# Second feed-forward projection of an encoder block: eight dense quarter products against seven block products

## The chip, the cores and the metric

The kernel runs on one core of one Trainium2 chip. The metric is device time in microseconds (us): the median of three timed runs. A separate execution was recorded by the hardware profiler; its page and its trace are what is read here.

TensorE (PE) multiplies a 128x128 stationary tile (loaded by PEld) with a moving tile of up to 512 columns into PSUM banks. VectorE (DVE), ScalarE (ACT) and GpSimd (POOL) work elementwise. SyncE's queue (SP) issues nearly all DMAs; a few are issued by ACT's queue.

## The reference, cut to what matters

One layer of a hybrid encoder on 1024 tokens of width 1024: an input layer norm, a wide projection, dilated attention and a gated recurrence, a merge, layer norm 1, and a SwiGLU feed-forward part with layer norm 2. The change lies in the last line and a half:

```
gate, up = jnp.split(h @ w_ffn_in[l], 2, axis=-1)
h = layer_norm(DEEPNORM_ALPHA * h + (jax.nn.silu(gate) * up) @ w_ffn_out[l], ln2_g[l], ln2_b[l])
```

The hidden width D_FF is 2816, which is 22 tiles of 128 (`NF`). The second projection therefore multiplies a 1024 x 2816 matrix (tokens by hidden) with a 2816 x 1024 matrix. All of it is float32.

## The kernel before

**Numbers in halves.** Each float32 operand is split into a high part rounded to the matmul's type and a low part that is the remainder (`split`: a cast on ACT, a subtraction on POOL or DVE). `mm3` then makes one product of three matmuls: high by high, high by low, low by high (lines 225, 226, 227 in the kernel before).

**First projection (`ffn_in`).** It makes the 22 hidden tiles one after the other, each for all 1024 tokens, by a seven-product block scheme (`wino_project`) of 7 x 4 x 3 = 84 matmuls per tile. An `evac` function turns the finished banks into the gated values `c` (tile `fc`), splits them (`fgh`, `fgl`) and stores both parts to DRAM (`gd`).

**Second projection (`ffn_out`).** It is dense. For the first four token tiles, eight PSUM banks (four tiles by two column halves) accumulate over all 22 hidden tiles; for each hidden tile `out_weights` loads a 512 KB row block of the weights into `w_raw` and splits it into `wohi`, `wolo`, which stay in SBUF, and `out_acts` loads the two stored parts of the activations (`gwsum`, `gwkeep`). For the last four token tiles the weights are there, and only activations are loaded. That makes 22 x 8 x 2 x 3 = 1056 matmuls. `finish` adds the banks to the residual row block `y` (loaded from `ahs`), takes the layer norm, and stores the output.

**Order.** The code is written as a stream of operations on tiles from rotating pools; a scheduler then sets each engine's instruction order ahead of time, by its own model of durations and by priorities. On the chip every engine runs its list strictly in order, and SP issues its DMAs strictly in order. A load is stopped at the queue's head until its buffer is free, and everything behind it waits too. The DMAs use eight completion semaphores in turn, so that at most eight are under way.

**Names.** `gwsum`, `gwkeep`: activations, high and low part, before. `Wb_...`: a 128x512 block of the weights, after. `graw`, `ghi`, `glo`: activations raw, high, low, after. `a22h`, `a22l`: high and low part of the last block's activations, after. `y`: residual rows, `ahs`: their copy in DRAM. `ga11f`, `gs4h` and the like: activation blocks in DRAM, after.

Of the kernel before, what the change touches and what calls it, by code (L numbers as in the profile page):

```python
# [25 lines left out]
NF = D_FF // 128  # L26
ALPHA = 2.0 ** 0.25
# [52 lines left out]
class Block:  # L80
    evac_ahead = 1000

    def __init__(self, ctx, tc, x, ln_in_g, ln_in_b, w_in, hgrn_lb, hgrn_norm_g, w_att_up, w_hgrn_up,
# [35 lines left out]
        self.gd = [[dram.tile([128, 4, T], F32, name=f"gd{i}{z}") for z in ("hi", "lo")] for i in range(6)]  # L119
# [1018 lines left out]
    def phase2(self):  # L1138
        nc = self.nc
        gc, bc = self.col["g1"], self.col["b1"]  # L1140
        with ExitStack() as es:
# [69 lines left out]
            for t in range(8):  # L1211
# [31 lines left out]
                if t in (5, 6):  # L1243
                    raws.append(self.ffn_raws(t - 5))
# [126 lines left out]
    def ffn_in(self):  # L1371

        nc = self.nc
        with ExitStack() as es:
# [3 lines left out]
            self.fp = fp = es.enter_context(self.pool("ffn", "right"))  # L1378

            def evac_of(f):  # L1380
                c, th = (fp.tile([128, T], F32, name=n, tag=n, bufs=2) for n in ("fc", "fth"))
                gh, gl = (fp.tile([128, T], F32R, name=n, tag=n, bufs=2) for n in ("fgh", "fgl"))

                def evac(i, l, ps, add):
# [11 lines left out]
                    self.split(gh[:, s], gl[:, s], c[:, s], eng_lo="dve")  # L1396
                    for t, d in zip((gh, gl), self.gd[f // 4]):
                        nc.sync.dma_start(d[:, f % 4, s], t[:, s].bitcast(F32))

                return evac  # L1400

# [5 lines left out]
            self.first_evac = [evac_of(f) for f in range(2)]  # L1407
            for i, n in enumerate(("b22", "t3", "t4")):
                for k in (0, 2):
                    tag = "fgh" if k else "fgl"  # L1410
                    r = fp.tile([128, 2, HALF], F32, name="t_raw", tag=tag, bufs=2)
                    nc.sync.dma_start(r, self.td[i][:, k:k + 2, :])
                    hi, lo = self.xb[n]
                    self.split(hi[:, k:k + 2, :], lo[:, k:k + 2, :], r, eng_lo="dve")
            ab = []
            held = None
            for f in range(NF):
                if f > 1:
                    grp = self.wino_project(nxt, evac_of(f))
                    next(grp)  # L1420
                else:
                    grp = self.first_groups[f]
                if 1 < f + 1 < NF:
                    nxt = self.ffn_raws(f + 1)
                if held:
                    next(held, None)
                next(grp)
                held = grp
                if f == 3:
                    for v in self.ln["1"]:  # L1430
                        vecs(v)
                if 5 <= f < 21 and f % 2:
                    t = f // 2 - 2
                    n = fp.tile([128, D], F32, name="res", tag="fc", bufs=2)
# [9 lines left out]
    def out_weights(self, f):  # L1444

        r = self.wraw.tile([128, D], F32, name="w_raw", tag="wraw", bufs=2)
        self.nc.sync.dma_start(r, self.wfo[128 * f:128 * (f + 1), :])
        if f < 2:
            t = [[z.rearrange("p k c -> p (k c)") for z in self.granules()] for _ in range(2)]
        else:  # L1450
            z = [self.fob.tile([128, D], F32R, name=f"wo{n}{f}") for n in ("hi", "lo")]
            t = [[y[:, HALF * h:HALF * (h + 1)] for y in z] for h in range(2)]
        for h, (hi, lo) in enumerate(t):
            self.split(hi, lo, r[:, HALF * h:HALF * (h + 1)], eng_lo="dve" if h else "pool")
        return t

    def out_acts(self, f, tk, n=4):

        out = []
        for i, tag in enumerate(("wsum", "wkeep")):  # L1460
            t = self.ws.tile([128, 4, 128], F32R, name=f"g{tag}", tag=tag, bufs=3)
            d = self.gd[f // 4][i]
            if tk.stop - tk.start == HALF:
                self.nc.sync.dma_start(t.rearrange("p k c -> p (k c)").bitcast(F32), d[:, f % 4, tk])
            else:
                self.nc.sync.dma_start(t[:, :n, :].bitcast(F32), d[:, 0:n, tk])
            out.append(t)
        return out

    def ffn_out(self):  # L1470
# [3 lines left out]
        with ExitStack() as es:  # L1474
            self.fob = es.enter_context(self.pool("fob"))
            rp = es.enter_context(self.pool("for", "right"))
            g2, b2 = (rp.tile([128, D], F32, name=n) for n in ("g2", "b2"))
            for t, v in zip((g2, b2), self.ln["2"]):
                nc.scalar.dma_start(t, bass.AP(tensor=v.tensor, offset=v.offset, ap=[[0, 128], [1, D]]))

            def finish(t, banks):
                y = rp.tile([128, D], F32, name="y2", tag="y2", bufs=2)
                nc.sync.dma_start(y, self.ahs_d[t])
                halves = [slice(HALF * h, HALF * (h + 1)) for h in range(2)]
                for s, ps in zip(halves, banks):
                    nc.vector.tensor_add(y[:, s], y[:, s], ps)
# [88 lines left out]
```

## Time and profile before

| | |
|---|---|
| Three runs | 2162.01, 2162.53, 2163.58 us; median 2162.53 |
| Profiled execution | span 2160.4 us from first to last instruction; its run time is not given apart, and the median of the runs is 2.1 us above the span |
| TensorE busy, share of the span | 2058.8 us, 95% |
| DVE, ACT, POOL busy | 1266.4, 883.3, 1108.9 us |
| DMA | 306.87 MB, mean 142 GB/s |
| Mean granted TensorE clock | 0.987 |

How to read it: busy times are sums over the whole span, and they say little about one stage. The second projection is the last tenth of the span, so the windows from about 1900 us on are the ones that bear on the change. The first projection fills about 1500 to 1911 us.

### The profile page before, as it was taken

The numbers are of one execution on the slowest core, as the hardware profiler recorded it, in microseconds if no ns is written. First come the engines' busy times: TensorE is split into PE (matmuls) and PEld (weight loads), VectorE is DVE, ScalarE is ACT, GpSimd is POOL, SyncE is SP. The second block draws the span as 40 slices with busy tenths as digits, with TensorE's granted clock in tenths as the row PEclk, the third lists the DMA queues.
The fourth block names the chain that finished last, engine by engine and source line by source line (L and its number), as shares of the span: only waits on it lengthen the run. The fifth ranks groups of instructions, "written<-read, shape, count | busy, mean of one in ns | idle before, by whom it ended". The sixth has DMA issues, their size and how long they took to land.

```text
span 2160.4 us, 31020 instructions
## 1 busy us (share of the span) xinstructions
PE 2058.8 (95%) x11073; PEld 1700.5 (79%) x11073; DVE 1266.4 (59%) x2037; ACT 883.3 (41%) x1798; POOL 1108.9 (51%) x905
## 2 busy tenths in 40 slices
PE   4799999999999999989999899998999999999998
PEld 3678887778878888778888688786888888887886
DVE  8667646876459854768446623247766776743221
ACT  6534455444544436444364431244444444432000
POOL 3565553566436763656635864443665666633120
PEclk9899999999999999999999999999999999999999
DMA  6343442434334453333525774245334444376452
GB/s 209 99 126 103 144 148 90 145 118 159 118 95 141 136 167 100 127 118 127 166 91 183 238 227 132 88 142 174 132 123 135 148 135 137 123 233 215 132 171 87
DMA packets 291644, 306.87 MB, mean 142 GB/s; under 512 B 14689, under 2 KB 222882, under 8 KB 291490
## 3 DMA queue, kind: packets, MB, share of 16 engines
q1 hardware_dynamic: 283744, 278.45, 40.7%
q10 hardware_dynamic: 7746, 26.45, 3.1%
q8 instruction: 87, 1.43, 0.3%
q14 instruction: 67, 0.55, 0.1%
HBM read 203.13 MB, written 101.71 MB: 141 GB/s over the span
## 4 chain that ended last, share of the span: by engine, by line
PE 61%; DVE 5%; DMA 4%; POOL 3%; issue 3%; ACT 1%; SPq 0%; DVEq 0%; POOLq 0%; ACTq 0%
PE pj L225 13%; PE pj L226 12%; PE pj L227 12%; PE sd L225 6%; PE sd L227 6%; PE sd L226 6%; POOL w_lo L204 2%; DMA w_raw<-in_w_ffn_out_dram 2%; PE sd L1019 1%; DVE hR L980 1%; DVE wolo L204 1%; DVE hR L979 1%; ACT wohi L200 0%; PE sd L557 0%; DMA wa<-in_w_in_dram 0%
## 5 line engine op out<-in xcount | busy, mean ns | idle before, releaser
L204 POOL TENSOR_TENSOR w_lo<-wa,w_hi 128x512 fp32r<-128x512 f32 x276 | 385.7, 1405 | 276.3 <-ACT w_hi L200 260.9
L200 ACT CAST w_hi<-wa 128x512 fp32r<-128x512 f32 x276 | 170.1, 618 | 231.7 <-PE pj L226 164.7
L204 POOL TENSOR_TENSOR w_lo<-wsum,w_hi 128x512 fp32r<-128x512 f32 x88 | 120.5, 1380 | 133.5 <-ACT w_hi L200 81.9
L225 PE MATMUL pj<-xt1hi,w_hi 128*128 128x512 f32 x268 | 109.1, 408 | 22.9 <-ACT xt1hi L200 15.3
L204 POOL TENSOR_TENSOR w_lo<-f_raw,w_hi 128x512 fp32r<-128x512 f32 x66 | 99.8, 1514 | 52.6 <-ACT w_hi L200 50.2
L226 PE MATMUL pj<-xt1lo,w_hi 128*128 128x512 f32 x268 | 107.9, 403 | 4.5 <-DVE xt1lo L204 4.5
L227 PE MATMUL pj<-xt1hi,w_lo 128*128 128x512 f32 x268 | 107.1, 400 | 0.0
L227 PE MATMUL pj<-xb22hi,w_lo 128*128 128x512 f32 x268 | 104.8, 391 | 1.8 <-POOL w_lo L204 1.8
L225 PE MATMUL pj<-xb22hi,w_hi 128*128 128x512 f32 x268 | 105.7, 394 | 0.4 <-ACT wkeep L1341 0.4
L226 PE MATMUL pj<-xb22lo,w_hi 128*128 128x512 f32 x268 | 104.9, 391 | 0.0
L459 POOL TENSOR_TENSOR wa<-wa,wa 128x512 f32<-128x512 f32 x46 | 65.4, 1422 | 72.4 <-DVE ws L458 61.0
L194 POOL TENSOR_TENSOR mv<-mv,mhalf 128x1 f32<-128x1 f32 x24 | 16.5, 689 | 162.8 <-DVE mv L193 159.6
L204 POOL TENSOR_TENSOR w_lo<-ws,w_hi 128x512 fp32r<-128x512 f32 x46 | 67.3, 1467 | 63.5 <-ACT w_hi L200 59.5
L200 ACT CAST w_hi<-wsum 128x512 fp32r<-128x512 f32 x88 | 54.6, 620 | 102.1 <-PE sd L226 67.2
L481 ACT COPY wkeep<-pj 128x512 f32<-128x512 f32 x138 | 80.4, 582 | 11.5 <-DVE evh L373 6.0
L225 PE MATMUL pj<-xb11hi,w_hi 128*128 128x512 f32 x188 | 77.6, 414 | 4.7 <-DVE wkeep L398 3.1
L225 PEld LDWEIGHTS pj<-xt1hi,w_hi 128*128 128x128 f32 x268 | 51.7, 194 | 36.7 <-ACT xt1hi L200 15.9
L225 PE MATMUL pj<-xt4hi,w_hi 128*128 128x512 f32 x188 | 75.8, 403 | 3.9 <-DVE evh L373 3.9
L384 DVE TENSOR_TENSOR evh<-wkeep,pj 128x512 f32<-128x512 f32 x48 | 32.7, 680 | 76.5 <-PE pj L227 56.3
L227 PE MATMUL pj<-xt2hi,w_lo 128*128 128x512 f32 x188 | 73.9, 393 | 3.3 <-POOL w_lo L204 3.3
L971 ACT ACTIVATE hS<-hR,dec 128x128 f32<-128x128 f32 x112 | 44.5, 402 | 79.4 <-DVE hR L980 56.3
L226 PE MATMUL pj<-xb11lo,w_hi 128*128 128x512 f32 x188 | 75.7, 403 | 1.0 <-DVE xb11lo L204 1.0
(396 smaller groups left out, 6517.7 us busy)
## 6 DMA issues: line engine op xcount, KB each, us to landing
wa<-in_w_in_dram SPq DMA_DIRECT2D x184, 256.0 KB, 3.1
f_raw<-in_w_ffn_in_dram SPq DMA_DIRECT2D x44, 512.0 KB, 4.1
w_raw<-in_w_ffn_out_dram SPq DMA_DIRECT2D x22, 512.0 KB, 3.6
tg<-evh SPq DMA_DIRECT2D x32, 256.0 KB, 3.0
tg<-tg SPq DMA_DIRECT2D x16, 512.0 KB, 3.8
y<-ahs SPq DMA_DIRECT2D x16, 512.0 KB, 3.7
ah<-xt ACTq DMA_DIRECT2D x8, 512.0 KB, 6.7
rec<-hg ACTq DMA_DIRECT2D x8, 512.0 KB, 3.6
```

Source lines behind the costliest of these rows:

```text
L200: nc.scalar.copy(hi, src)
L204: e.tensor_sub(lo, src, hi.bitcast(F32))
L225: nc.tensor.matmul(ps, whi, xhi, start=first, stop=False, **kw)
L226: nc.tensor.matmul(ps, whi, xlo, start=False, stop=False, **kw)
L227: nc.tensor.matmul(ps, wlo, xhi, start=False, stop=last, **kw)
L384: nc.vector.tensor_add(t, add, ps)
L459: nc.gpsimd.tensor_sub(a["a21"], a["a11"], a["a21"])
L481: nc.scalar.copy(t, ps)
L971: nc.scalar.activation(S[:, c, :], E, AF.Copy, scale=dec[:, 1, c:c + 1])
L979: nc.vector.scalar_tensor_tensor(En, E, dec[:, 1, c:c + 1], ps[:, jj, :], op0=OP.mult, op1=OP.add)
L980: nc.vector.tensor_scalar(En, En, dec[:, 0, c:c + 1], None, op0=OP.mult)
L1019: nc.tensor.matmul(po[:, jj, :], l, r, start=(n == 0), stop=(n == len(terms) - 1))
```

## The change

The dense second projection is replaced by a seven-product block scheme, like that of the first projection. The activations are seen as 2 x 2 blocks (hidden tiles j and j + 11, token halves), the weights too, and the 22 hidden tiles become 11 pairs (`NJ`). Seven products over 11 pairs, each for four token tiles and 512 columns, make 7 x 11 x 4 x 3 = 924 matmuls.

- `ffn_in` now makes the hidden tiles in the order 0, 11, 1, 12, ... (`FS`), so that a pair is complete after two. A new `combine` makes the four block sums of the activations: `s3` (POOL) after the first tile of a pair, `s1`, `s2`, `s4` (DVE) after the second. It stores `a11`, `a12`, `s2` whole and `s3`, `a22`, `s1`, `s4` as two parts: 11 stores of 256 KB per pair where there were 8.
- The last three tables of the first projection (`b22`, `t3`, `t4`) are fetched in 12 loads of 256 KB instead of 6 of 512 KB.
- `ffn_out` runs the products in the order 1, 2, 6, 5, 7, 3, 4. Every one but the last takes 11 steps of 12 matmuls. Products 1, 6, 7 and 4 use one set of four banks (`X`, the `pj` banks), 2, 5 and 3 the other (`Z`, the `sd` banks).
- All 44 weight blocks stay in SBUF as raw float32; `right` forms the sums of weights in place on DVE, and each step splits its weight block anew (ACT and POOL). `a11`, `a12`, `s2` are loaded raw and split on arrival; `s1`, `s3`, `s4` are loaded as two parts.
- All eight `y` rows stay in SBUF, and after each product the banks are added straight into them.

```diff
-            self.first_out = self.out_weights(0), self.out_acts(0, slice(0, HALF))
             next(held, None)
+            combine(NJ - 1, 1)
...
+            def combine(j, second):
+                a11, a21 = (C[j][:, HALF * l:HALF * (l + 1)] for l in range(2))
+                if not second:
+                    whole("a11", j, a11)
+                    s3 = small("s3")
+                    nc.gpsimd.tensor_sub(s3, a11, a21)
+                    parts("s3", j, s3)
+                    return
+                a12, a22 = (C[j + NJ][:, HALF * l:HALF * (l + 1)] for l in range(2))
+                whole("a12", j, a12)
+                parts("a22", j, a22)
+                s1, s2, s4 = (small(n) for n in ("s1", "s2", "s4"))
+                nc.vector.tensor_add(s1, a21, a22)
+                nc.vector.tensor_sub(s2, s1, a11)
+                nc.vector.tensor_sub(s4, a12, s2)
...
+    OUT_ORDER = (1, 2, 6, 5, 7, 3)
...
+            def acts(p, j):
+                d = self.gd[self.OUT_G[p]][j]
+                z = [rp.tile([128, HALF], F32R, name=f"g{n}", tag=f"g{n}", bufs=3) for n in ("hi", "lo")]
+                if len(d) == 1:
+                    r = self.ws.tile([128, HALF], F32, name="graw", tag="wsum", bufs=3)
+                    nc.sync.dma_start(r, d[0])
+                    self.split(*z, r, eng_lo="dve")
+                else:
+                    for t, s in zip(z, d):
+                        nc.sync.dma_start(t.bitcast(F32), s)
+                return z
+
+            def right(p, j):
...
+                if p == 6:
+                    t2 = self.ws.tile([128, HALF], F32, name="wt2", tag="wkeep", bufs=3)
+                    nc.vector.tensor_sub(b11, b12, b11)
+                    nc.vector.tensor_sub(t2, b22, b11)
+                    return t2
...
+            for j in range(NJ):
+                load("b11", j)
...
+            for p in self.OUT_ORDER:
+                bank = X if p in (1, 6, 7) else Z
+                for j in range(NJ):
+                    if p == 1:
+                        load("b21", j)
+                        if j in (3, 5, 7, 9):
+                            rows((j - 3) // 2)
+                    if p == 2:
+                        load("b12", j)
...
+                    g = acts(p, j)
+                    w = self.granules()
+                    w = [z.rearrange("p k c -> p (k c)") for z in w]
+                    self.split(*w, right(p, j))
...
+                    for t in range(4):
+                        c = slice(128 * t, 128 * (t + 1))
+                        self.mm3(bank[t], g[0][:, c], g[1][:, c], *w, p in (1, 2, 5) and j == 0, j == NJ - 1,
+                                 skip_group_check=True)
...
+            for t in range(4):
+                for j in range(NJ):
+                    self.mm3(X[t], a22[t][0][:, j, :], a22[t][1][:, j, :], *late[j], False, j == NJ - 1,
+                             skip_group_check=True)
+                add(4 + t, 0, X[t])
+                finish(t)
             for t in range(4, 8):
+                finish(t)
```

The order of the instructions moves with it. Three places matter for what follows.

SP's queue at the end of the first projection, before: the first activations and weights of the second projection stand between the last stores (`gd5hi`, `gd5lo`) of the first.

```order
L1398 DMA gd5hi<-fgh 128x512
L1398 DMA gd5lo<-fgl 128x512
L1464 DMA gwsum<-gd0hi 128x512 x2
L1398 DMA gd5hi<-fgh 128x512
L1398 DMA gd5lo<-fgl 128x512
L1464 DMA gwkeep<-gd0lo 128x512
L1447 DMA w_raw<-in_w_ffn_out_dram 128x1024
```

The same place after, where `gs1h`, `gs2f`, `gs1l`, `ga12f`, `gs4h` are stores of the last pair:

```order
L1414 DMA gs1h_255<-gh 128x512
L1408 DMA gs2f_234<-s_17476 128x512
L1414 DMA gs1l_256<-gl 128x512
L1408 DMA ga12f_223<-fc 128x512
L1493 DMA Wb_17504<-in_w_ffn_out_dram 128x512
L1493 DMA Wb_17506<-in_w_ffn_out_dram 128x512
L1414 DMA gs4h_299<-gh 128x512
```

Three activation loads (`graw` of steps 0 to 2) stand ahead of this piece, but the first weight block now stands behind the store `ga12f_223`, whose data comes from the very last product of the first projection.

SP's queue some 15 us into the second projection, before: two loads of weights and two of activations take turns.

```order
L1447 DMA w_raw<-in_w_ffn_out_dram 128x1024 x2
L1464 DMA gwsum<-gd1hi 128x512
L1464 DMA gwkeep<-gd1lo 128x512
L1447 DMA w_raw<-in_w_ffn_out_dram 128x1024 x2
L1464 DMA gwsum<-gd1hi 128x512
```

The corresponding stretch after, from the activations of step 8 (`ga11f_210`) to those of step 9 (`ga11f_211`):

```order
L1504 DMA graw<-ga11f_210 128x512
L1493 DMA Wb_18246<-in_w_ffn_out_dram 128x512
L1493 DMA Wb_18273<-in_w_ffn_out_dram 128x512
L1497 DMA y_18400<-ahs_119 128x1024
L1497 DMA y_18444<-ahs_120 128x1024
L1497 DMA y_18488<-ahs_121 128x1024
L1497 DMA y_18532<-ahs_122 128x1024
L1597 DMA a22h<-ga22h 128x11x128
L1597 DMA a22l<-ga22l 128x11x128
L1597 DMA a22h<-ga22h 128x11x128
L1597 DMA a22l<-ga22l 128x11x128
L1504 DMA graw<-ga11f_211 128x512
```

The last two of the 44 weight blocks, the rows of the second token half (asked for by the code in product 5) and half of the activations of product 4 have moved ahead of the activations of step 9 of product 1.

DVE's list near the start of the second projection, before: subtractions of weights (`wolo`), which wait only for their own block.

```order
L204 TENSOR_TENSOR fgl<-fc,fgh 128x512
L204 TENSOR_TENSOR wolo_17317<-w_raw,wohi_17316 128x512
L204 TENSOR_TENSOR wolo_17353<-w_raw,wohi_17352 128x512
L204 TENSOR_TENSOR wolo_17389<-w_raw,wohi_17388 128x512
L204 TENSOR_TENSOR wolo_17425<-w_raw,wohi_17424 128x512
```

DVE's list after, from a sum of weights for product 6 (line 1519) to the low part of the activations of step 6 of product 1 (`glo`):

```order
L1519 TENSOR_TENSOR Wb_17520<-Wb_18002,Wb_17520 128x512
L1520 TENSOR_TENSOR wt_18094<-Wb_18004,Wb_17504 128x512
L1526 TENSOR_TENSOR Wb_17810<-Wb_18004,Wb_17810 128x512
L1519 TENSOR_TENSOR Wb_17522<-Wb_18028,Wb_17522 128x512
L1520 TENSOR_TENSOR wt_18121<-Wb_18030,Wb_17506 128x512
L1526 TENSOR_TENSOR Wb_17834<-Wb_18030,Wb_17834 128x512
L208 TENSOR_TENSOR glo<-graw,ghi 128x512
```

The sums for products 6 and 7 have moved into product 1, and a `glo` behind them waits until their weight blocks have landed.

More of the change, by code (lines that the diff above doesn't have):

```diff
@@ L26 @@
 NF = D_FF // 128
+NJ = NF // 2
+FS = [j + NJ * z for j in range(NJ) for z in range(2)]
 ALPHA = 2.0 ** 0.25
@@ L118, in __init__ @@
         self.td = [dram.tile([128, 4, HALF], F32, name=f"td{i}") for i in range(3)]
-        self.gd = [[dram.tile([128, 4, T], F32, name=f"gd{i}{z}") for z in ("hi", "lo")] for i in range(6)]
+        self.gd = {n: [[dram.tile([128, HALF], F32, name=f"g{n}{z}{j}") for z in zs] for j in range(NJ)]
+                   for n, zs in (("a11", "f"), ("a12", "f"), ("s2", "f"), ("s1", "hl"), ("s3", "hl"), ("s4", "hl"))}
+        self.gd["a22"] = [dram.tile([128, NJ, HALF], F32, name=f"ga22{z}") for z in "hl"]
         self.consts()
@@ L1378, in ffn_in @@
             self.fp = fp = es.enter_context(self.pool("ffn", "right"))
+            C = {}
             def evac_of(f):
-                c, th = (fp.tile([128, T], F32, name=n, tag=n, bufs=2) for n in ("fc", "fth"))
-                gh, gl = (fp.tile([128, T], F32R, name=n, tag=n, bufs=2) for n in ("fgh", "fgl"))
+                C[f] = c = fp.tile([128, T], F32, name="fc", tag="fc", bufs=4)
+                th = fp.tile([128, T], F32, name="fth", tag="fth", bufs=2)
                 def evac(i, l, ps, add):
@@ L1438, in ffn_in @@
                     nc.scalar.dma_start(self.ahs_d[t], n)
-            self.first_out = self.out_weights(0), self.out_acts(0, slice(0, HALF))
             next(held, None)
+            combine(NJ - 1, 1)
         self.rawpool.__exit__(None, None, None)
         self.h1p.__exit__(None, None, None)
[L1444 to L1468, printed above, removed]
+    OUT_ORDER = (1, 2, 6, 5, 7, 3)
+    OUT_G = {1: "a11", 2: "a12", 6: "s2", 5: "s1", 7: "s3", 3: "s4"}
     def ffn_out(self):
@@ new lines, in ffn_out, with load, rows @@
+            halves = [slice(HALF * h, HALF * (h + 1)) for h in range(2)]
+            def load(n, j):
+                W[n, j] = t = wb.tile([128, HALF], F32, name=f"W{n}", tag=f"{n}{j}", bufs=1)
+                k, c = int(n[1]) - 1, int(n[2]) - 1
+                nc.sync.dma_start(t, self.wfo[128 * (j + NJ * k):128 * (j + NJ * k + 1), HALF * c:HALF * (c + 1)])
+            def rows(t):
+                Y[t] = y = rp.tile([128, D], F32, name="y2", tag=f"y2{t}", bufs=1)
+                nc.sync.dma_start(y, self.ahs_d[t])
@@ L1487, in finish, with add @@
+            def add(t, h, ps):
+                with self.tc.high_priority(offset=self.evac_ahead):
+                    nc.vector.tensor_add(Y[t][:, halves[h]], Y[t][:, halves[h]], ps)
+            def finish(t):
+                y = Y[t]
                 mv = self.stats(rp, y, "2")
@@ new lines, in ffn_out @@
+            a22 = []
+            for t in range(4):
+                a22.append([rp.tile([128, NJ, 128], F32R, name=f"a22{z}", tag=f"a22{z}", bufs=2) for z in "hl"])
+                for z, d in zip(a22[t], self.gd["a22"]):
+                    nc.sync.dma_start(z.bitcast(F32), d[:, :, 128 * t:128 * (t + 1)])
+            for t in range(4):
[4 more added lines that the diff above has]
+                finish(t)
```

120 lines of the change are left out of this document (63 added, 57 removed).

## The prediction

> **What bounds the kernel now.** I read the page first, then the windows of the stages, the waits of PE, PE's timeline at both ends of the second projection, and the DMA slices.
>
> ```profile
> span 2160.4 us, 31020 instructions
> PE 2058.8 (95%) x11073; PEld 1700.5 (79%) x11073; DVE 1266.4 (59%) x2037; ACT 883.3 (41%) x1798; POOL 1108.9 (51%) x905
> PE 61%; DVE 5%; DMA 4%; POOL 3%; issue 3%; ACT 1%; SPq 0%; DVEq 0%; POOLq 0%; ACTq 0%
> ```
>
> PE is busy for 95% of the span and carries the chain. The windows are the first projection (without its start) and the second; columns are PE, PEld, DVE, ACT, POOL, clock, DMA share, GB/s.
>
> ```profile
> 1530.00:1900.00 370.00, 370.00 (x1634) 306.37 (x1633) 253.56 (x248) 158.72 (x273) 222.63 (x155) 1.00 0.41 133
> 1911.00:2152.00 241.00, 240.12 (x1057) 197.75 (x1056) 65.33 (x84) 33.40 (x51) 47.64 (x35) 1.00 0.54 172
> ```
>
> Both are PE's at full granted clock (1.00). The waits of PE after 1911 us are 0.9 us in all:
>
> ```profile
> PE sd L225 <- ACT wohi L200: 0.7, 1, 0.7
> PE sd L225 <- DMA gwsum<-gd3hi: 0.2, 1, 0.2
> ```
>
> So every matmul removed is worth its pitch, as long as PE stays fed.
>
> ```profile
> 1902.88 0.39 PE L225 MATMUL pj<-xb22hi,w_hi 128*128 128x512 f32 x1
> ...
> 2144.21 0.39 PE L226 MATMUL pj<-wolo,gwsum 128*128 128x512 f32 x1
> ...
> 2151.92 0.39 PE L227 MATMUL pj<-wohi,gwkeep 128*128 128x512 f32 x1
> ```
>
> The last two rows are 34 matmuls apart: 7.71/34 = 0.2268 us each (the 0.39 us overlap). From the first row on, 36 matmuls of the first projection are left; so E, the point where its work alone would end, is 1902.88 + 36 x 0.2268 = 1911.0 us. The last matmul ends its turn at 2151.92 + 0.23 = 2152.15. Before, E to end takes 241.1 us: 1056 x 0.2268 = 239.5, and 1.6 of idle.
>
> **The gain.** 1056 - 924 = 132 matmuls x 0.2268 = 29.9 us less work for PE, all on the path.
>
> **The price: PE is not fed in product 1.** A step is now 12 x 0.2268 = 2.72 us. Prices of what feeds it:
>
> ```profile
> L204 DVE TENSOR_TENSOR wolo<-w_raw,wohi 128x512 fp32r<-128x512 f32 x20 | 27.3, 1363 | 38.8 <-ACT wohi L200 37.1 <-DMA gwkeep<-gd3lo 1.8
> L204 POOL TENSOR_TENSOR wolo<-w_raw,wohi 128x512 fp32r<-128x512 f32 x20 | 25.9, 1293 | 46.0 <-ACT wohi L200 44.2 <-DMA gwkeep<-gd3lo 1.8
> L200 ACT CAST wohi<-w_raw 128x512 fp32r<-128x512 f32 x40 | 22.8, 618 | 42.7 <-DMA w_raw<-in_w_ffn_out_dram 42.7
> L1486 DVE TENSOR_TENSOR y<-y,sd 128x512 f32<-128x512 f32 x8 | 5.4, 681 | 61.5 <-PE sd L227 60.2 <-DMA y<-ahs 1.3
> L1501 DVE TENSOR_TENSOR y<-y,b 128x1024 f32<-128x1024 f32 x7 | 10.7, 1537 | 20.5 <-POOL y L1500 20.5
> ```
>
> A POOL subtraction (1.29) and one or two casts (0.62 each) fit into 2.72 us. The loads are what does not. In SP's order after, the activations of step 9 stand behind all 44 weight blocks, all eight `y` rows, half of `a22` and the last stores. From the first weight block to those activations: 44 x 0.262 MB = 11.5; two stores `gs4`, 0.5; eight rows of 0.524, 4.2; four `a22` loads of 128 x 11 x 128 floats, 2.9; seven raw activation blocks, 1.8; and on ACT's queue the two 512 KB vectors, 1.05. Sum 22.0 MB. PE could do the nine steps before it in 24.5 us, so the load rate decides. Its rows, a stretch with 2 KB and 4 KB runs (1912 to 1918 us), one with the 512-byte runs of `f_raw` (1405 to 1415 us), and a ten-us mean with lulls:
>
> ```profile
> DMA  9799999999999999999999999999999987654333
> GB/s 355 287 410 423 423 382 423 437 423 382 451 437 437 410 410 437 437 369 396 410 423 369 423 396 382 423 382 423 410 410 382 369 314 287 259 219 191 150 137 123
> DMA  0000016578578999999999999999999999999999
> GB/s 0 0 0 0 0 47 90 150 219 221 117 184 231 270 270 406 440 369 485 369 356 342 336 367 334 332 330 324 299 291 295 287 291 289 293 289 313 338 319 358
> 1920.00:1930.00 10.00, 10.00 (x46) 8.29 (x45) 2.49 (x3) 2.28 (x4) 2.35 (x3) 1.00 0.93 331
> ```
>
> Where the engines are at 9 tenths and 2 KB or 4 KB runs flow, the slices lie about 410; with 512-byte runs, between 290 and 340. The 331 has lulls in which the queue was empty, and the burst has none. I take 400 for 19.1 MB (47.9 us) and 310 for the 2.9 MB of `a22`, which has 512-byte runs (9.3 us): 57.2 us. Bounds: 437 (the plateau's common top) and 385 give 43.7 + 7.5 = 51.2; 331 and 290 give 57.7 + 9.9 = 67.6.
>
> ```profile
> gwkeep<-gd0lo SPq DMA_DIRECT2D x6, 256.0 KB, 7.2
> gwsum<-gd5hi SPq DMA_DIRECT2D x2, 256.0 KB, 2.9
> 1914.56 0.32 SPq L1398 DMA_DIRECT2D gd5lo<-fgl  x1
> ```
>
> A lone 256 KB load lands 2.9 us after issue, of which 0.65 is data at 400 GB/s, so 2.25 us are fixed; the same load lands after 7.2 us with others ahead of it, so a load does wait for those before it. An issue takes 0.32 us.
>
> When does the burst start? Before, weights for the second projection were fetched among the last stores and PE mixed both projections' matmuls. After, the first weight block stands behind the store of `a12`, which needs the last product. DVE has six operations of 0.68 us to do from the end of the product before it (2.7 us before E), so until E + 1.4; then the last gating, 0.69, E + 2.1; two issues, E + 2.75. ACT's list casts three weight blocks before the first activations, so PE starts at about E + 9.4 (five DMAs with 1 MB of stores ahead, 5.3 us, and two casts); this idle is inside what follows.
>
> Step 9's activations land at E + 2.75 + 57.2 + 2.25 = E + 62.2, and are cast by E + 62.8. From there 68 of the 77 steps are left: 68 x 2.72 = 185.1, which ends at E + 247.9. Against 241.1 that is **+6.8 us** (with the bounds +0.8 to +17.2): a wait of some 38 us has eaten the gain of 29.9 and the 1.6.
>
> DVE's list holds a second wait inside this one: `glo` of step 6 stands behind 14 sums of weights that need ten blocks of `b12` and two of `b22`. They land just before the activations of step 6 (12.8 MB into the burst), so it costs nothing of its own; if the burst were faster, it would.
>
> **Smaller terms.**
>
> ```profile
> 1929.08 1.29 POOL L204 TENSOR_TENSOR wolo<-w_raw,wohi 128x512 fp32r<-128x512 f32 x1 [4.53 <-ACT wohi L200]
> 1929.56 1.36 DVE L204 TENSOR_TENSOR wolo<-w_raw,wohi 128x512 fp32r<-128x512 f32 x1 [4.46 <-ACT wohi L200]
> L204 DVE TENSOR_TENSOR fgl<-fc,fgh x41: 679/1773/1786, 1525.5 to 1895.2; 128x512 fp32r<-128x512 f32 x41
> ```
>
> DVE's subtraction of two SBUF tiles takes 0.68 alone and 1.36 to 1.77 beside POOL's. Product 2 now has three such operations of DVE (two sums of weights and `glo`) beside one of POOL in each step. DVE has 28 such operations there (19.0), eleven delays by POOL of 0.87 (midway between 1.36 - 0.68 and 1.77 - 0.68), 9.6, and four additions of 0.69, 2.8: 31.4 us for PE's 29.9, +1.5 (0, if the four-deep weight buffers cover it, to 3.4). The Trainium skill, SBUF — State Buffer, section Who interferes with whom, says that a DVE instruction with two SBUF inputs contends with a GpSimd one that reads SBUF and that the later fully blocks. The row agrees: DVE ends 0.55 us after POOL. By that rule a step takes 1.29 + 3 x 0.68 = 3.33 us, and product 2 would cost 11 x 0.61 = 6.7 instead of 1.5.
>
> First projection: per pair (38.1 us) DVE gets three sums and POOL one, SP three more stores; ACT's and DVE's four splits stay. DVE goes from 253.6/370 = 69% by 3 x 0.68 to 1.77 to 74 to 82%. PE shows 370.00 of 370 there, so this is cover, but evacuations queue behind sums that wait for POOL or for a store: +2, from 0 to 16 (1.5 us in each of 11 pairs). The twelve smaller `t_raw` loads carry the same bytes: nothing.
>
> Product 4: `a22` for token tiles 2 and 3 can be fetched only when tiles 0 and 1 are done; 1.44 MB at 310 GB/s is 4.7 us, plus 2.25, within the 7.5 us of a tile's 33 matmuls, unless output stores share the queue: +1 (0 to 3). Products 5, 7, 3 load two parts with a lead of two steps, 5.4 us, over 2.9: nothing.
>
> Tail: the chain after the last matmul stays, but DVE's list has the 128x1024 addition for row 6 (1.54 us) between the two halves of the last row's norm: +1.4. The additions into resident rows read PSUM (0.68 each), and lie beside PE.
>
> ```profile
> 2152.34 0.69 DVE L1486 TENSOR_TENSOR y<-y,pj 128x512 f32<-128x512 f32 x1 [2.66 <-PE pj L227]
> 2153.07 0.69 DVE L190 BATCH_NORM_STATS2 bn<-y 128x6 f32<-128x512 f32 x1
> 2155.50 1.41 DVE L1495 SCALAR_TENSOR_TENSOR y<-y,mv,b 128x512 f32<-128x512 f32 x2
> 2156.27 1.01 SPq L1497 DMA_DIRECT2D out_dram<-y  x2
> ```
>
> Sum: 6.8 + 1.5 + 2 + 1 + 1.4 = +12.7 us. The profiled span, 2160.4, becomes 2173.1; the runs' median lies 2.1 above the span, so **2175 us**.
>
> The Trainium skill, DMA: Bandwidth & Descriptors, section Where 436 GB/s comes from, says that for HBM to SBUF the HBM side binds at about 358 GB/s per core. The plateau of 410 speaks against it here; by 358 the burst takes an estimated 61.5 us, and the time would be 2179.
>
> **Rivals.**
>
> *Faster: the burst does not stop PE.* If the activations of step 9 came when needed, only the start (9.4 us) and the small terms would stand against the gain: 9.4 - 29.9 - 1.6 + 5.9 = -16.2, so 2146. For: nothing in the arithmetic of the products needs those rows and blocks so early. Against: the queue's order, and the 7.2 us row. It decides where step 9 can start before E + 45.8 (62.8 - 12.7 - 4.3): 22 MB in 40 us, 549 GB/s, above any plateau shown.
>
> *Level.* The burst runs at the plateau's top (+0.8) and the small terms are covered: about 2163 to 2166. For: 0.15 us slices of 437 to 451. Against: they do not last.
>
> *Much slower: the first projection loses its cover* at 1.5 us a pair: 2175 + 14 = 2189. For: the 1.77 us rows, DVE's order. Against: PE at 370.00 of 370, with a four-deep buffer of weight splits.
>
> **How the numbers follow.** A measurement of this kernel can tell about 0.2%, 4.3 us, from no change. The main case, 2167 to 2187 by the bounds of rates and small terms, has 0.62; the level one 0.16; the faster one 0.14; the much slower one 0.08. Slower: 0.62 + 0.08 = 0.70; within 0.2%: 0.16; faster: 0.14. The range 2158 to 2190 leaves out the faster case and a little beyond the slow one.
>
> **What would show it.** Right: PE with a gap of 7 to 10 us at the start of the second projection, then short steps and two long waits in product 1, before step 6 and before step 9, 12 to 14 us each; DMA share at 9 tenths for about 60 us; PE's pitch unchanged; the last 68 steps near 2.72 us. Wrong: activations of step 9 landing before `a22` (order not kept), slices well off 400 GB/s (rate), PE gaps within 1530 to 1900 us (first projection), or steps of product 2 over 3 us (POOL and DVE).

## The result, and the profile after

The changed kernel takes 2185.8 us (median of 4 runs, 2184.1 to 2187.3) against 2162.3 for the kernel before on the same chip: a ratio of 1.0102, 95% interval 1.0088 to 1.0117. It is 23.5 us slower; 12.7 were forecast, 2175, and the main case reached from 2167 to 2187. The profiled execution, the slowest of the four, has a span of 2185.5 us, 25.1 more than before.

From the page of the changed kernel: span, busy times, and the chain of work that ended last.

```profile
span 2185.5 us, 31268 instructions
PE 2037.5 (93%) x10941; PEld 1677.8 (77%) x10941; DVE 1380.8 (63%) x2165; ACT 920.1 (42%) x1870; POOL 1217.8 (56%) x960
PE 59%; DVE 6%; POOL 4%; DMA 4%; issue 4%; ACT 1%; SPq 1%; DVEq 0%; POOLq 0%; ACTq 0%
```

PE has 132 matmuls less, as the change says, and the span still grew: PE waits. Its waits after 1500 us (us in total, how many, the longest):

```profile
PE pj L229 <- ACT ghi L204: 35.1, 4, 12.2
PE pj L229 <- ACT xt1hi L204: 8.7, 1, 8.7
PE sd L229 <- DVE fu L1399: 2.4, 2, 1.6
PE sd L229 <- ACT w_hi L204: 0.5, 1, 0.5
```

The 8.7 us stand ahead of the first projection in both kernels (8.69 before). PE's rows at the seam of the two projections (start, duration; in brackets the idle time before and what ended it):

```profile
1920.11 0.39 PE L231 MATMUL sd<-xt4hi,w_lo 128*128 128x512 f32 x1
1929.74 0.80 PE L229 MATMUL pj<-w_hi,ghi 128*128 128x512 f32 x1 [9.24 <-ACT ghi L204]
1942.48 0.50 PE L229 MATMUL pj<-w_hi,ghi 128*128 128x512 f32 x1 [1.87 <-ACT ghi L204]
1963.11 0.80 PE L229 MATMUL pj<-w_hi,ghi 128*128 128x512 f32 x1 [12.15 <-ACT ghi L204]
1986.23 0.80 PE L229 MATMUL pj<-w_hi,ghi 128*128 128x512 f32 x1 [11.86 <-ACT ghi L204]
2173.36 0.39 PE L231 MATMUL pj<-t4hi,a22l 128*128 128x512 f32 x1
```

The first row is the last matmul of the first projection, so E is 1920.34. Product 1 starts 9.4 us later and stops before step 3 (1.87), step 6 (12.15) and step 9 (11.86), counted from 0. PE works on to 2173.59, and 11.9 us are left to the end. The queue of SP shows why step 9 waits (a row sums up to 14 issues; the duration is that of the issuing):

```profile
1945.06 11.56 SPq L1493 DMA_DIRECT2D Wb<-in_w_ffn_out_dram  x14
1957.02 0.33 SPq L1504 DMA_DIRECT2D graw<-ga11f  x1
...
1965.09 2.40 SPq L1497 DMA_DIRECT2D y<-ahs  x4
...
1969.39 6.83 SPq L1597 DMA_DIRECT2D a22h<-ga22h  x1
1976.26 2.39 SPq L1597 DMA_DIRECT2D a22l<-ga22l  x1
1978.75 2.81 SPq L1504 DMA_DIRECT2D graw<-ga11f  x2
```

The activations of steps 9 and 10 are issued at 1978.75, behind all weights, rows and half of `a22`. The windows of the burst (PE, PEld, DVE, ACT, POOL, clock, DMA share, GB/s):

```profile
1922.00:1930.00 8.00, 0.26 (x1) 0.26 (x2) 1.03 (x3) 3.30 (x6) 2.69 (x3) 0.67 0.99 336
1930.00:1945.00 15.00, 13.13 (x47) 10.32 (x48) 5.22 (x5) 4.45 (x8) 7.00 (x5) 0.84 1.04 397
1945.00:1963.00 18.00, 5.96 (x27) 4.60 (x25) 10.87 (x15) 2.94 (x5) 3.85 (x3) 0.79 1.05 389
1963.00:1970.00 7.00, 6.89 (x18) 5.46 (x19) 6.25 (x11) 1.81 (x4) 0.62 (x1) 0.57 1.05 395
1970.00:1985.00 15.00, 4.38 (x20) 3.27 (x18) 6.92 (x8) 1.24 (x2) 3.25 (x3) 0.81 1.13 322
2010.00:2040.00 30.00, 30.00 (x133) 24.37 (x132) 30.00 (x36) 12.28 (x23) 16.11 (x11) 1.00 0.36 98
```

The DMA engines are full for 63 us and move 23.2 MB (GB/s times length, summed; the share adds up the packets' times, so it can pass 1). The last row is product 2: PE is fed, though DVE is busy for 30.00 of 30.

The end, DVE's rows around the end of the last matmul, and one of POOL's:

```profile
2173.12 1.23 DVE L1551 TENSOR_TENSOR y<-y,b 128x1024 f32<-128x1024 f32 x1 [1.56 <-POOL y L1550]
...
2174.34 0.68 DVE L1533 TENSOR_TENSOR y<-y,pj 128x512 f32<-128x512 f32 x1
...
2175.77 2.34 POOL L1550 TENSOR_TENSOR y<-y,g 128x1024 f32<-128x1024 f32 x1 [2.17 <-ACT y L252]
2176.16 3.16 DVE L1542 SCALAR_TENSOR_TENSOR y<-y,mv,g 128x512 f32<-128x512 f32 x2
2179.24 1.21 DVE L1551 TENSOR_TENSOR y<-y,b 128x1024 f32<-128x1024 f32 x1
2180.38 1.40 DVE L1545 SCALAR_TENSOR_TENSOR y<-y,mv,b 128x512 f32<-128x512 f32 x2
```

Two additions of other rows (L1551) stand in the last row's chain, and its two products with `g2` take 3.16 us where the last two with `b2` take 1.40: POOL multiplies row 6 at the same time.

### The profile page after: what moved, and what is told of

The parts are those of the page before. It is cut to its first block, busy times and chain, and to the rows that moved or that the text cites. A ratio compares the mean times of both kernels' runs of the same rounds, so it can differ in the third digit from the quotient of the medians.

```text
span 2185.5 us, 31268 instructions
## 1 busy us (share of the span) xinstructions
PE 2037.5 (93%) x10941; PEld 1677.8 (77%) x10941; DVE 1380.8 (63%) x2165; ACT 920.1 (42%) x1870; POOL 1217.8 (56%) x960
## 4 chain that ended last, share of the span: by engine, by line
PE 59%; DVE 6%; POOL 4%; DMA 4%; issue 4%; ACT 1%; SPq 1%; DVEq 0%; POOLq 0%; ACTq 0%
PE pj L229 12%; PE pj L230 12%; PE pj L231 12%; PE sd L231 6%; PE sd L229 6%; PE sd L230 6%; POOL w_lo L208 2%; DMA Wb<-in_w_ffn_out_dram 1%; PE sd L1023 1%; DVE hR L984 1%; DVE hR L983 1%; DMA wa<-in_w_in_dram 1%; DMA graw<-ga11f 1%; DVE qd L938 0%; SPq L1597 0%
## 5 line engine op out<-in xcount | busy, mean ns | idle before, releaser
L208 POOL TENSOR_TENSOR w_lo<-wsum,w_hi 128x512 fp32r<-128x512 f32 x88 | 135.7, 1553 | 78.3 <-ACT w_hi L204 40.9
L208 POOL TENSOR_TENSOR w_lo<-f_raw,w_hi 128x512 fp32r<-128x512 f32 x66 | 109.0, 1664 | 66.6 <-ACT w_hi L204 65.5
L208 POOL TENSOR_TENSOR w_lo<-Wb,w_hi 128x512 fp32r<-128x512 f32 x55 | 74.2, 1350 | 119.3 <-ACT w_hi L204 114.1
L229 PE MATMUL pj<-xt1hi,w_hi 128*128 128x512 f32 x268 | 109.2, 408 | 22.0 <-ACT xt1hi L204 15.7
L229 PE MATMUL pj<-w_hi,ghi 128*128 128x512 f32 x132 | 55.1, 418 | 35.1 <-ACT ghi L204 35.1
L1393 ACT ACTIVATE fth<-fc 128x512 f32<-128x512 f32 x44 | 27.8, 632 | 122.3 <-DVE fc L1392 122.3
```

Of the source, the lines that this page charges most:

```text
L208: e.tensor_sub(lo, src, hi.bitcast(F32))
L229: nc.tensor.matmul(ps, whi, xhi, start=first, stop=False, **kw)
L1393: nc.scalar.activation(th[:, s], c[:, s], AF.Tanh, scale=0.5)
```

## The experiments

All kernels below are edits of the changed kernel. Stages are compared by PE's rows: "first" runs from the first matmul that reads the stage's `xt1` (1498.89 before) to the end of the first projection's last matmul, "second" from there to the end of the last matmul, "tail" from there to the end of the span. This is needed because the stage starts between 1495.1 and 1503.1 us in executions whose earlier code is the same, so a span alone says a few us too much or too little. The rows are those of one execution of each kernel; the medians come from several chips, on which the kernel before takes 2162.3 to 2164.9, so across kernels the ratios are to be compared.

| kernel | start | first | second | tail | span | median | ratio to before, 95% |
|---|---|---|---|---|---|---|---|
| before | 1498.9 | 412.1 | 241.1 | 8.3 | 2160.4 | 2162.3 | 1 |
| changed | 1502.6 | 417.8 | 253.3 | 11.9 | 2185.5 | 2185.8 | 1.0102 (1.0088 to 1.0117) |
| e1 late loads | 1498.4 | 417.1 | 247.7 | 16.0 | 2179.1 | 2181.0 | 1.0086 (1.0066 to 1.0105) |
| e2 more burst | 1500.8 | 418.6 | 259.2 | 11.8 | 2190.4 | 2189.9 | 1.0128 (1.0111 to 1.0146) |
| e3 early start | 1498.4 | 421.1 | 246.0 | 11.6 | 2177.2 | 2178.7 | 1.0076 (1.0058 to 1.0094) |
| e4 tail | 1498.0 | 418.4 | 255.1 | 13.5 | 2184.9 | 2186.9 | 1.0113 (1.0092 to 1.0134) |
| e5 late, held | 1505.5 | 426.9 | 237.4 | 15.2 | 2185.0 | 2187.1 | 1.0111 (1.0096 to 1.0127) |
| e6 tail, rows first | 1501.9 | 416.7 | 253.8 | 10.5 | 2182.8 | 2182.2 | 1.0087 (1.0073 to 1.0101) |
| e7 s3 on DVE | 1495.1 | 415.3 | 254.3 | 11.6 | 2176.2 | 2183.5 | 1.0085 (1.0072 to 1.0098) |
| e8 combined | 1506.1 | 429.9 | 228.2 | 13.8 | 2177.9 | 2182.4 | 1.0087 (1.0073 to 1.0102) |
| e9 held, other place | 1503.1 | 416.5 | 237.2 | 15.7 | 2172.4 | 2175.6 | 1.0048 (1.0035 to 1.0061) |
| e10 combined 2 | 1500.5 | 419.7 | 233.4 | 14.6 | 2168.2 | 2168.7 | 1.0016 (1.0007 to 1.0025) |
| e11 combined 3 | 1498.2 | 420.3 | 230.9 | 7.6 | 2156.9 | 2157.8 | 0.9971 (0.9961 to 0.9981) |
| e12 combined 4 | 1498.8 | 418.2 | 231.1 | 7.6 | 2155.8 | 2157.2 | 0.9966 (0.9954 to 0.9978) |

In e3, e8 and e10 to e12 up to two steps of the second projection, 5.4 us, run inside "first".

**More burst.** Is it the bytes ahead in the queue that step 9 waits for?

```diff
                     if p == 2:
                         load("b12", j)
+                        if j < 8:
+                            x = rp.tile([128, HALF], F32, name="Wx", tag=f"x{j}", bufs=1)
+                            nc.sync.dma_start(x, self.wfo[128 * j:128 * (j + 1), HALF:D])
```

> Eight more blocks of 0.262 MB that nobody reads are loaded among the weight blocks of product 2's stretch of the program, 2.1 MB. Theory (the bytes ahead in the queue set when step 9 starts): at 400 GB/s 5.2 us longer, 2191 us, and the wait before step 9 or step 6 grows by as much. Rival (step 9 waits for something else, the casts of ACT or the sums of DVE, or the queue has slack): no change, 2186.

Start to last matmul grew by 6.7 us (417.8 + 253.3 to 418.6 + 259.2), the wait before step 9 from 11.86 to 18.06; the medians are 4.1 apart. The queue has no slack: the theory holds, with its 5.2 between the two.

**Early start.** Is the 9.4 us gap a cost of its own, or inside the burst's wait?

```diff
+            self.pre = self.first_steps()
             next(held, None)
             combine(NJ - 1, 1)
...
+    # first_steps: blocks b11 0..3 into two wraw tiles; raw a11 0 and 1; both steps split
```

> The first four blocks of b11 and the first two activation blocks are loaded, and two steps split, while the first projection still runs; the rest of the burst keeps its order. Theory (the start gap lies inside the burst's wait): PE starts right after the first projection instead of 9.4 us after it, but steps 6 and 9 only wait longer; the burst has 6 blocks, 1.6 MB, less, at 390 GB/s 4.0 us: 2182 us. Rival (the start gap is a cost of its own): 9.4 us less, 2176.

Start to last matmul is 4.0 us shorter (667.1 instead of 671.1), the theory's 4.0 and not 9.4. PE's gap moved: its waits are now 6.73, 5.41, 9.42 and 9.12 us, 30.7 in all instead of 35.1. The medians alone would not decide it: they differ by 7.1 us, between theory and rival. Of the spans' 8.3, 4.2 are an earlier start of the stage.

**Late loads.** Then the order of the queue should be worth the whole wait.

```diff
+            def hold(v):
+                if seen:
+                    nc.scalar.copy(v, seen[-1][:, 0:1].bitcast(F32))
             def load(n, j):
                 W[n, j] = t = wb.tile(...)
+                hold(t[:, 0:1])          # so the load follows the step before
...
+                    if p == 3 and j in (4, 6):
+                        a22_load(j // 2 - 2)
```

> Every load that product 1 does not need at once (the blocks b21, b12 and b22, the rows of y, the first two pairs of a22) is held back until a step shortly ahead of its use: the activations of steps 6 and 9 then no longer stand behind the rest of the burst. Theory (the order of SP's queue starves product 1): the waits of 12.2, 1.9 and 11.9 us go, and about 1.5 us of low clock behind them with them; PE's start, 9.4 us after the first projection, stays. 2185.8 - 27 = 2159 us. Rival A (product 1 is short of bytes whatever their order): 41 blocks of 0.262 MB and 1 MB of stores at 390 GB/s take 30 us, PE would wait for 5 to 10 us spread over steps 3 to 11: 2164 to 2169. Rival B (DVE, busy for 10 of 10 us in product 2, becomes the bound once the waits no longer let it run ahead): steps of product 2 over 3 us, 2165 or more.

A miss, and the most useful one. The waits before steps 6 and 9 are gone, but the second projection is only 5.6 us shorter. DVE's windows and PE's waits in that kernel:

```profile
1965.00:1975.00 10.00, 8.90 (x40) 7.01 (x39) 9.90 (x15) 3.72 (x10) 4.89 (x3) 1.00 0.48 146
...
1985.00:1995.00 10.00, 9.75 (x44) 7.76 (x43) 10.00 (x14) 3.38 (x8) 3.23 (x2) 1.00 0.56 180
1995.00:2005.00 10.00, 7.20 (x31) 5.18 (x29) 10.00 (x13) 3.81 (x8) 4.62 (x3) 1.00 0.47 154
2005.00:2015.00 10.00, 5.34 (x14) 4.07 (x14) 10.00 (x17) 2.33 (x6) 2.41 (x3) 0.66 0.27 84
```

```profile
PE pj L231 <- DVE glo L208: 8.7, 3, 4.7
PE sd L231 <- DVE glo L208: 3.2, 3, 1.8
```

The third pair in a window is DVE's: full from 1965 to 2015. Its groups between 1925 and 2035 say with what (mean ns behind the comma):

```profile
L208 DVE TENSOR_TENSOR glo<-graw,ghi 128x512 fp32r<-128x512 f32 x33 | 30.1, 932 | 28.8 <-ACT ghi L204 24.4 <-PE pj L231 4.5
L1532 DVE TENSOR_TENSOR Wb<-Wb,Wb 128x512 f32<-128x512 f32 x11 | 11.7, 1061 | 0.3 <-DMA Wb<-in_w_ffn_out_dram 0.2
L1536 DVE TENSOR_TENSOR Wb<-Wb,Wb 128x512 f32<-128x512 f32 x11 | 9.9, 907 | 0.1
L1539 DVE TENSOR_TENSOR Wb<-Wb,Wb 128x512 f32<-128x512 f32 x11 | 9.7, 878 | 0.0
L1541 DVE TENSOR_TENSOR Wb<-Wb,Wb 128x512 f32<-128x512 f32 x11 | 9.6, 877 | 0.0
```

The sums of products 5, 7 and 3 (L1536, L1539, L1541; 29 us) need only weights, so DVE's list has them as soon as the blocks are there, tens of us before their use and ahead of the `glo` that PE needs next. In the changed kernel PE was waiting for loads meanwhile. Rival B was right: the waits for `glo` are 11.9 us. They are not the whole of what is missing. PE also waits 3.0 us for `a22`, which is now loaded late, and 1.5 us for the activations of product 5, and the tail is 4.1 us longer.

**Late loads, sums held.** The sums are tied to the step before by a factor 1.0 made from its activations.

```diff
+                one = self.tiny.tile([128, 1], F32, name="one", tag="one", bufs=3)
+                v = seen[-1][:, 0:1].bitcast(F32)
+                nc.vector.tensor_tensor(one, v, v, op=OP.is_equal)
                 if p == 5:
-                    nc.vector.tensor_add(b21, b21, b11)
+                    nc.vector.scalar_tensor_tensor(b21, b21, one, b11, op0=OP.mult, op1=OP.add)
...                                      # products 7 and 3 likewise
```

> As the kernel with the late loads, and the in-place sums of weights of products 5, 7 and 3 are held too: each multiplies one operand by a 1.0 that DVE makes from the activations of the step before, so that none can be done 30 us ahead of its use. Theory (with the loads late, DVE's sums for four products, all run ahead inside products 2 and 6, made the activations' subtractions late, and ate the gain): DVE falls well under 10 of 10 us between 1965 and 2015, the waits for glo (11.9 us and the slow matmuls) go, and only the 9.4 us at the start stays: 77 steps of 2.72 us and 9.4 make 219 us from the end of the first projection to the last matmul instead of the 247.6 with late loads: 2155 to 2160. Rival (bytes or the DVE and POOL contention bound product 2 in any order): 2170 or more.

A miss by the clock, but not in the stage: the second projection fell to 237.4 us, 15.9 under the changed kernel and 3.7 under before (219 was expected; beside the 9.1 at the start, waits of 0.5 to 2.7 us remain, with slow matmuls behind some of them). The waits for `glo` went from 11.9 to 2.8 us. What undid it was the first projection, 426.9 instead of 417.1, and its stage began later as well, though PE runs the same matmuls in the same order as with late loads alone. What had changed there was addresses, and the next experiment takes that up.

**The same, the tile in another place.**

```diff
-                one = self.tiny.tile([128, 1], F32, name="one", tag="one", bufs=3)
+                one = rp.tile([128, HALF], F32, name="one", tag="one", bufs=3)[:, 0:1]
```

> The kernel with late loads and held sums once more; only the place of the small tile of 1.0 differs: not in the pool of statistics, which lies below nearly every other pool, where its 12 bytes moved every address behind it, but in a pool of the second projection alone. In the last experiment the first projection, whose instructions and order were unchanged, took 39.2 us a pair instead of 38.4, with every third matmul 0.24 us after the one before instead of 0.227. Theory (the moved addresses cost that, not the held sums): pairs are 38.4 us again, the first projection's end comes 9 us earlier after the start of its stage, the second one's steps are 2.72 us again, 6 us less: 2187 - 9 - 6 - 5 (the stages before) = 2167 us. Rival (the held sums or the late loads cost it): pairs stay at 39.2, 2187.

The same 340 us of the first projection, first with the tile in the low pool, then in the other (count of PE's matmuls in the first brackets):

```profile
1560.00:1900.00 340.00, 340.00 (x1459) 273.53 (x1458) 277.72 (x249) 138.25 (x242) 232.35 (x147) 1.00 0.45 150
...
1560.00:1900.00 340.00, 339.86 (x1490) 278.78 (x1489) 280.39 (x256) 140.84 (x250) 244.88 (x151) 1.00 0.46 153
```

1459 matmuls against 1490, both with PE busy within 0.2 us of the whole and at full granted clock. The first projection is back at 416.5, so the theory holds there; the two combined kernels below repeat it, with 1459 matmuls (tile in the low pool) and 1501 in this window. The second one stayed at 237.2: its steps had not been slowed, and with the 6 us counted for that missing 2175.6 is measured instead of 2167. The tail, 15.7 us, is now the worst part.

**The tail.** Two orders for the norms.

```diff
             for t in range(4):
+                finish(t)                # e4: one row ahead of each tile; e6: all four ahead of product 4
                 for j in range(NJ):
                     self.mm3(X[t], a22...)
                 add(4 + t, 0, X[t])
-                finish(t)
-            for t in range(4, 8):
-                finish(t)
+                finish(4 + t)
-                if t == 7:               # in finish: fused operations of DVE alone
+                if t > 5:
```

> Rows 0 to 3 are normed beside product 4, each row from 4 on as soon as its last addition is done, and row 6, like row 7, with DVE's fused operations alone. Theory (row 6's norm on ACT, POOL and DVE stands between the halves of row 7's): the span from the last matmul's end to the end falls from 11.9 us to about 8.3, and the time to 2182. Rival (the end is the chain of row 7 alone, and the rest lies beside it): no change, 2186.

> Against the changed kernel only the end differs: the norms of rows 0 to 3, complete after product 3, are all written ahead of product 4; rows 4 to 6 follow their last addition; row 6 like row 7 by DVE alone. Theory (an addition of another row, 1.2 us, and a POOL product that slows DVE, stood inside row 7's chain in the changed kernel and still did in the first tail experiment, there those of row 3): last matmul to end 8.3 instead of 11.9 us, time 2182.5. Rival (the rest of the chain and the stores decide): 11 us or more, 2185 to 2187.

The first order left the additions of row 3 in the last chain: 13.5 us, worse. The second gives 10.5 us, between theory and rival, and 2182.2 us in time, the theory's number; but the tail has only 1.4 us of the 3.6 that were to go, so that agreement is in part luck.

**s3 on DVE.** `nc.gpsimd.tensor_sub(s3, a11, a21)` becomes `nc.vector.tensor_sub`.

> The subtraction that makes s3 in the first projection moves from POOL to DVE. Theory (POOL's extra 1.3 to 1.75 us per pair makes the split of the first weights of product 3 late; PE loses 0.33 us a pair, 2.6 us in eight pairs): pairs are 38.08 us apart again, 2183. Rival (DVE's three sums cause it): pairs stay at 38.4 us or get longer, 2186 or more.

The same 340 us, the changed kernel above and this one below:

```profile
1560.00:1900.00 340.00, 339.81 (x1490) 278.83 (x1489) 280.05 (x256) 140.44 (x248) 244.64 (x150) 1.00 0.46 153
...
1560.00:1900.00 340.00, 340.00 (x1502) 281.62 (x1501) 275.10 (x265) 140.67 (x249) 222.96 (x144) 1.00 0.46 153
```

1502 matmuls is what before has there. The 12 that were missing, 2.7 us, were POOL's doing, and the time fell to 2183.5 as the theory said (the ratios' intervals overlap; the counts decide). Note that 339.81 "busy" of 340 hid this loss: the lost pieces, 0.11 and 0.18 us, hardly pass the overlap of the matmuls' durations (0.39 - 0.23 = 0.16). The count shows it.

**Combined.** The parts together, first with the 1.0 still in the low pool, then with it moved, a third `a22` buffer, and DVE-only norms for rows 3 to 7.

> Late loads, held sums, early first steps, the row norms ahead of product 4, and s3 on DVE together. Theory: 2157 (late loads and held sums) less 6 to 7 at the start, 3.5 at the end and 2.6 in the pairs: 2144 to 2147, under both kernels. Rival (the parts trade one wait for another, as the late loads alone did): 2155 to 2165.

> All that helped, with the tile of 1.0 in that other place: late loads, held sums, the first two steps loaded and split ahead, s3 on DVE; a third buffer for a22 and its loads four to eight steps earlier; rows 0 to 3 normed ahead of product 4 and rows 3 to 7 by DVE's fused operations alone, so that POOL's products, which slow DVE, end early. Theory: 2167 less 7 at the start, 2.6 in the pairs, 4 in waits for a22 and 4 at the end: 2149, under both kernels. Rival (DVE, with sums, subtractions and norms, is the bound at the end, and waits only move): 2160 or more.

Both missed. The first is 36 us above its theory, of which the slower first projection found above (429.9) is about 10. The second is at 2168.7 instead of 2149, in its rival's range: the second projection is 233.4, and DVE holds the end. The window from 2130 to 2160 us, and below it that of the third combined kernel, whose span ends at 2156.9:

```profile
2130.00:2160.00 30.00, 23.74 (x105) 19.33 (x103) 29.96 (x53) 3.62 (x3) 13.65 (x10) 0.96 0.45 153
...
2130.00:2160.00 30.00, 19.51 (x87) 15.81 (x85) 16.23 (x30) 0.00 (x0) 3.38 (x4) 0.88 0.31 101
```

**Combined, product 3 ahead of product 7.**

```diff
-    OUT_ORDER = (1, 2, 6, 5, 7, 3)
+    OUT_ORDER = (1, 2, 6, 5, 3, 7)   # rows 0 to 3 are complete after product 3
...
+                if p == 3:
+                    for t in range(4):
+                        finish(t)
```

> The second combined kernel with product 3 ahead of product 7, so that rows 0 to 3 are complete 30 us earlier and their norms lie beside product 7; rows 4 to 7 are normed by DVE alone, with POOL idle; the sums of product 7 are made in product 5; a22 is loaded in halves of 0.72 MB through product 7; the last seven blocks of b11 are loaded three steps ahead of their use; activations have four buffers instead of three. Theory (in the second combined kernel DVE, busy for 30.0 of 30 us between 2130 and 2160, held the end: eight rows' additions and norms in the last 37 us): DVE falls under 25 of 30 there, last matmul to end falls from 14.6 us to 8 to 9, the waits for a22 and for loads behind it, 5 us, go: 2168.7 - 6 - 5 = 2158, and up to 4 less at the start. Rival (DVE and POOL's total work bounds the second projection in any order): 2165 or more.

DVE falls from 29.96 to 16.23 us in that window, the tail to 7.6 us, and the time to 2157.8: the theory's number, and faster than before by 0.29% (0.19 to 0.39%). The kernel has the expectation's other edits too (norms of rows 4 to 7 without POOL, sums of product 7 in product 5, `a22` in halves, four activation buffers, late `b11`); how much each brought was not taken apart.

**Combined, b11 later.** What is left at the start: ACT casts two weight blocks, still under way, ahead of activations that have landed.

```diff
                     if p == 1:
-                        if 0 < j < NJ - 3:
-                            load("b11", j + 3)
+                        for i in {3: (4, 5, 6), 4: (7,), 5: (8,), 6: (9,), 7: (10,)}.get(j, ()):
+                            load("b11", i)
```

> As the third combined kernel, but the blocks of b11 for steps 4 to 10 are loaded only from step 3 on, so that ACT's casts of them no longer stand ahead of the casts of the activations of steps 2 and 3, which have landed. In the third combined kernel PE still waited 9.3 us before step 2 and 4.2 us before step 4. Theory (ACT's order holds the start; the activations are there): the first wait falls to the time until the last stores of the first projection have left their tiles, 4 to 6 us, the second stays within 2 to 5 us because the blocks now arrive later: 2157.8 - 4 = 2154. Rival (the second projection's tiles come free no earlier): the first wait stays at 9 us and the second grows: 2158 to 2161.

PE's waits between 1917 and 1950 us, third combined kernel, then this one:

```profile
PE pj L229 <- ACT ghi L204: 13.5, 2, 9.3
```

```profile
PE pj L229 <- ACT w_hi L204: 6.3, 1, 6.3
PE pj L229 <- ACT ghi L204: 5.3, 2, 2.7
```

The wait before step 2 fell to 2.7 us, so ACT's order did hold it, but a new one of 6.3 us stands before step 4, for the blocks now loaded later. The time, 2157.2, is the same within the intervals; 2154 was the theory.

## Why the prediction was right, and where it was short

The sign, the mechanism and its place were right: the queue's order, not PE, sets the start of step 9, with waits before steps 6 and 9. The size was half of what came, and some terms met their rows by luck. Each term against the rows:

| term | forecast | measured |
|---|---|---|
| before the first projection's stage | 0 | +3.7 |
| first projection | +2 | +5.7 |
| start of product 1 after E | 9.4 | 9.4 |
| waits before steps 6 and 9 | 12 to 14 each | 12.2 and 11.9 |
| step 9 after E | 62.8 | 65.9 |
| last 68 steps, with the terms of products 2 and 4 | 187.6 | 187.4 |
| tail | +1.4 | +3.7 |
| span | +12.7 | +25.1 |

*Step 9* is 3.1 us late. The first block is issued 1.7 us after E rather than 2.75, but issue to cast takes 63.5 us rather than 59.5: 23.2 MB flow instead of the 22.0 counted (the last pair's stores, issued just ahead, were left out but for two), at 336 GB/s in the first 8 us and 389 to 397 in the next 40, where 400 was taken. The Trainium skill's 358 GB/s for the HBM side (DMA: Bandwidth & Descriptors, Where 436 GB/s comes from) does not bind here: 40 us stand above it. That the prediction's estimate by it, 61.5 us for the burst, comes nearer to the measured 63.5 is chance, since it was worked out for 22.0 MB.

*The start of product 1* is met by luck: the first block was issued 1.0 us earlier than forecast, and the third one's cast began 6.5 us after that (1928.55) instead of 5.3, a figure that the prediction does not work out; the two cancel in the 9.4.

*Products 2 and 4* cost next to nothing: PE 30.00 of 30. That 187.4 meets 187.6 is luck. 68 steps are 185.1, and of the other 2.3 us 1.7 are the first eight matmuls after the wait before step 9, which take 3.48 us (1986.23 to 1989.71) instead of 1.81; the prediction had no such term. Nor is the reason that it gave for a cost of 0, four-deep buffers, what the runs show. DVE had done sums during PE's waits; with the waits gone (late loads) it held PE for 11.9 us. The rule of the Trainium skill, SBUF — State Buffer, section Who interferes with whom, that a DVE instruction with two SBUF inputs and a GpSimd one that reads SBUF exclude each other, agrees with the rows (the sums' means of 877 to 1061 ns against 680 alone). What it costs PE by itself no run took apart: holding the sums back brought the waits for `glo` down to 2.8 us with POOL's instructions as they were. (The prediction's 0.87 us for one such delay is 0.885 midway, which is 0.2 us in its sum.) The faster rival, 2146 if the loads came in time, was priced too well: the late loads alone give 2181, and DVE's waits are the largest part of the difference that has a name.

*First projection.* +2 was taken out of 0 to 16 on the sign of PE's 370.00 of 370. It was 5.7: 2.7 us are POOL's subtraction for `s3`, shown by moving it. The other 3 lie at the stage's start and end (waits for `fu` and `w_hi`, and low clock behind a wait); between executions these vary (416.5 to 418.6 among kernels with the same first projection), and no run took them apart.

*Tail.* Mis-sized in its step "the chain after the last matmul stays, +1.4": it counted one addition in the list, not that all eight rows are normed in the last 41 us (DVE's first statistics of a row start at 2144.98), with POOL's products beside DVE. In the third combined kernel four rows are done beside product 7 and the others without POOL; with that, its tail is 7.6 us where the second combined kernel has 14.6.

*Before the stage.* 3.7 us of the span's 25.1 lie in code that did not change, within the spread of the starts above; the runs' medians, 23.5 apart, hold less of it.

## What to carry to other kernels

When PE gets less work, list for each other engine and queue what it now does per step, and in which order its list runs it; a wait that you remove may be the cover under which another engine did its work. In-place sums and large loads that depend on nothing run as early as the list allows, so tie them to the step that needs them, and finish output rows early enough that their norms do not meet at the end. Compare stages by landmarks and counts of matmuls, not by "busy" shares and spans.

## What the runs showed of the hardware

A tile of 4 bytes per partition in three buffers, put into a pool below nearly all others, moved addresses, and PE did 1459 instead of 1490 matmuls in the same 340 us: the same matmuls in the same order, all "busy", at a granted clock of 1.00. The first matmuls of two pairs, with the addresses moved and then with the tile elsewhere:

```profile
1651.38 0.39 PE L229 MATMUL pj<-xt1hi,w_hi 128*128 128x512 f32 x1
1690.58 0.39 PE L229 MATMUL pj<-xt1hi,w_hi 128*128 128x512 f32 x1
```

```profile
1644.22 0.39 PE L229 MATMUL pj<-xt1hi,w_hi 128*128 128x512 f32 x1
1682.62 0.39 PE L229 MATMUL pj<-xt1hi,w_hi 128*128 128x512 f32 x1
```

A pair is 39.20 us, without a gap, instead of 38.40, which holds 0.33 of waiting for POOL: over its 168 matmuls a pitch of 0.2333 instead of 0.2266. (In the trace's nanoseconds two of three starts are 0.231 apart and the third 0.238: every matmul is slower, not every third alone, as the expectation reads.) It cost 10.4 us in the first projection (426.9 against 416.5). That it is the addresses is inferred, from the edit that moves nothing else; which tile's address does it was not tried.

PE's first matmuls after a long wait are slow: here behind the 9.3 us wait in the third combined kernel, with a window inside the wait (clock 0.50):

```profile
1924.00:1926.00 2.00, 0.00 (x0) 0.00 (x0) 0.00 (x0) 0.55 (x1) 1.26 (x1) 0.50 1.00 294
```

```profile
1927.88 0.79 PE L229 MATMUL pj<-w_hi,ghi 128*128 128x512 f32 x1 [9.27 <-ACT ghi L204]
1928.48 0.63 PE L230 MATMUL pj<-w_lo,ghi 128*128 128x512 f32 x1
...
1931.04 0.63 PE L230 MATMUL pj<-w_lo,ghi 128*128 128x512 f32 x1
...
1933.16 0.39 PE L229 MATMUL pj<-w_hi,ghi 128*128 128x512 f32 x1
```

They are 0.43 us apart (six pitches in 2.56 us) where 0.227 is the rule. The twelve matmuls from 1927.88 to 1933.16 take 5.28 us instead of 2.72, so this wait costs 2.6 us beyond its length; the one before step 9 of the changed kernel costs 1.7. Shorter waits can do it too: with late loads the matmuls from 1.5 us behind a wait of 1.84 us (ended 1979.01) are 0.43 apart for 3 us, at a clock of 0.51, while behind one of 2.80 (ended 1999.23) none is.
